# Splitting the weights once: block 0 stores the fp32r pairs in DRAM, and blocks 1 to 3 load them

## The chip, the core and the metric

The kernel runs on one core of one Trainium2 chip. The metric is the device time of one execution in microseconds. Before the change it was 3058.07 us, the median of three runs.

## The reference

One layer of a streaming encoder is applied to 2048 prompt rows and 32 sample rows of width 1024. What matters here is that every row goes through the same weights:

```
h = RMSNorm(x);  proj = h @ w_in          # 1024 x 9760: q k v, gates, z, x B C, dt
branch_a = (window_attention(q, k, v) * silu(g_att)) @ w_attn_o
branch_s = (ssd_scan(conv(xBC), dt) * silu(z), grouped RMSNorm) @ w_ssm_o
out = (sigmoid(ga) * branch_a + sigmoid(gs) * branch_s) @ w_out
x  <- x + RMSNorm(out)
```

## The kernel before

The 2048 rows are cut into four blocks of 512 columns (the tokens lie along the free axis). Block 1 also carries the 32 sample rows, so its matmuls run in two parts of 272 columns. The scan state and the last rows of convolution and keys pass from block to block.

A float32 product is made of three fp32r matmuls: each operand is split into a rounded part (hi) and the rest (lo), and hi*hi, hi*lo and lo*hi are summed in PSUM. The activations are split where they are made. The weights are split by `prep`, in every block again.

The projections of a block are a list of 125 jobs, and the four lists stand one behind the other in `jobs`. A job makes 128 output channels. A *whole job* has eight slices of 128 rows of weights and so 24 matmuls of 512 columns; a *half job* (the 32 jobs of `ssm_out`, which multiply by `w_ssm_o` group by group) has four slices and 12 matmuls. The first job of a block (`dt`, marked `mix`) holds both parts in one tile. `emit_job` writes a job's matmuls on TensorE; `half_of` holds the matmul itself (L142). Everything else, the scan of a group (`load`, `prepare` and `finish` for each chunk of 128 tokens), attention, and the norms, is a list of side steps that `advance` places between the matmuls of the jobs, one step for each whole job or two half jobs.

Each side step takes PSUM tiles from the pool `sd` (four buffers). In the scan, `finish` takes three of them (y0, y, pst) and the `prepare` that follows takes two (pb, ps), so the transposes of x into ps (L437) wait until VectorE has read the y0 of that `finish` (L479, which writes into `ee`).

Weights in the loop over jobs:

```
while done_load < min(nj, j + 1 + LOOK_DMA):    # LOOK_DMA = 4
    load_raw(done_load); done_load += 1
while done_prep < min(nj, j + 1 + LOOK):        # LOOK = 2
    prep(done_prep); done_prep += 1
```

`load_raw` brings 512 KB (a whole job, or two half jobs) into one of three `raw` buffers. `prep` copies it on ScalarE to fp32r (`whi`, L123) and subtracts on VectorE (`wlo`, L127); there are three buffers of each, so the pair of job j+2 can be written only when the matmuls of job j-1 are done. All DMAs are issued by SyncE, one queue in program order: a DMA that waits holds up every DMA behind it. In the scan, `load` brings the chunk's rows of the decay from a small DRAM tile, 512 KB into `rr` and 256 KB into `ee` by two DMAs (three buffers of each), so such a load waits for the `finish` that read the buffer before. The order of each engine's instructions is fixed when the program is built, by the framework's scheduler.

Of the kernel before, what the change touches and what calls it, by code (L numbers as in the profile page):

```python
# [7 lines left out]
F32 = mybir.dt.float32  # L8
F32R = mybir.dt.float32r
# [5 lines left out]
P = 128  # L15
# [14 lines left out]
LOOK_DMA = 4  # L30
# [3 lines left out]
def hybrid_step_kernel(ctx: ExitStack, tc: tile.TileContext, ins, outs):  # L34
# [6 lines left out]
    wp = pool("wp", 3)  # L41
# [4 lines left out]
    sm = pool("sm", 4)  # L46
    dram = pool("dram", 2, space=bass.MemoryType.DRAM)
    mm = pool("mm", 4, space=bass.MemoryType.PSUM)
    sd = pool("sd", 4, space=bass.MemoryType.PSUM)

    act, vec, pl, pe = nc.scalar, nc.vector, nc.gpsimd, nc.tensor
    dma = nc.sync.dma_start

    # ---------------------------------------------------------------- constants
    cst = const.tile([P, 3, P], F32, name="cst")
# [6 lines left out]

    # ---------------------------------------------------------------- state kept over blocks
    H = const.tile([P, 4, 512], F32, name="H")
# [12 lines left out]

    # ---------------------------------------------------------------- helpers
    def rsqrt(x, n, rows=P):
# [14 lines left out]

    # ---------------------------------------------------------------- weights
    jobs = []
    raws = {}

    def raw_key(j):
        return jobs[j]["raw"]  # L100
# [10 lines left out]

    prepped = {}

    def prep(j):
        load_raw(j)
        jb = jobs[j]
        rv = raws[raw_key(j)]
        o = jb["off"]
        kt = jb["load"][1]
        src = rv[:, :, o:o + P]  # L120
        hi = wp.tile([P, 1024], F32R, name="whi")[:, :kt * P].rearrange("p (k c) -> p k c", k=kt)
        lo = None if jb["mix"] else wp.tile([P, 1024], F32R, name="wlo")[:, :kt * P].rearrange("p (k c) -> p k c", k=kt)
        act.activation(hi, src, AF.Copy)  # L123
        if jb["mix"]:
            vec.tensor_tensor(hi[:, :, 32:64], src[:, :, :32], hi[:, :, :32].bitcast(F32), op=ALU.subtract)
        else:
            vec.tensor_tensor(lo, src, hi.bitcast(F32), op=ALU.subtract)  # L127
        prepped[j] = (hi, lo)

# [83 lines left out]

    # ---------------------------------------------------------------- one block
    def block(b):
# [12 lines left out]

        # ---- input norm and transposition
        def stage_a(io):  # L230
# [64 lines left out]

        # ---- dt
        def evac_dt(res):
# [63 lines left out]

        # ---- conv channels
        def evac_conv(ci, dst):
# [32 lines left out]

        # ---- state space scan of one group
        def ssd_steps(g, ph):
# [190 lines left out]

        # ---- attention  # L590
        def att_open(ph):
# [111 lines left out]
        def att_unit(kv, ph):  # L703
# [18 lines left out]
            def softmax(sps, pt, rng_, neg, n):  # L722
                # rng_: per column i the (source AP, destination AP, max group)
                mx = sm.tile([P, 4], F32, name="mx")
# [260 lines left out]

    # ---------------------------------------------------------------- plan
    blocks = [block(b) for b in range(NB)]
# [31 lines left out]
    for b in range(NB):  # L1019
# [57 lines left out]
        add_jobs(w_ou, KT, 0, 8, tb, bk["rhs_m"], [bk["evac_out"](d) for d in range(8)], name=("outs", b))  # L1077
        jobs[-5]["after"].append((f"o{b}", bk["out_steps"](ph)))

    # ---------------------------------------------------------------- run  # L1080
    open_phase("io", 9)()
    for slot in blocks[0]["stage_a"](ph):
        for f in slot:
            f()
    # ---------------------------------------------------------------- small parameters
    load_raw(0)
# [98 lines left out]
    for j in range(nj):  # L1185
# [5 lines left out]
        if "ensure" in jb:  # L1191
            nm, key = jb["ensure"]
            for side in list(active):
                while side[0] == nm and key not in finished:
                    advance(side, True)
        while done_load < min(nj, j + 1 + LOOK_DMA):
            load_raw(done_load)
            done_load += 1
# [79 lines left out]
```

## Time and profile before

| | |
|---|---|
| time, median of 3 runs | 3058.07 us (3057.89 to 3060.25) |
| span of the profiled execution, first to last instruction | 3055.3 us |
| TensorE busy | 2977.4 us |
| VectorE busy | 2146.2 us |
| ScalarE busy | 1445.6 us |
| GpSimd busy | 587.2 us |
| moved by DMA | 323.40 MB, 106 GB/s in the mean |
| granted clock of TensorE, mean | 0.995 |

The span is 2.8 us shorter than the median time; what lies around it is the launch and the end. "Busy" counts the time in which at least one instruction of the engine ran, and the idle time of an engine is the rest of the span. TensorE is idle for 77.9 us of 3055.3.

### The profile page before, as it was taken

What the parts mean: (1) busy time and instruction counts of PE and PEld (TensorE: products, weight loads), DVE (VectorE), ACT (ScalarE), POOL (GpSimd) and SP (SyncE); (2) the same over time, 40 slices, a digit from 0 to 9 for tenths busy, and PEclk for the clock granted to TensorE, in tenths of its full rate; (3) what the DMA queues carried; (4) which work ended last, traced back from release to release, by engine and by line L of the source; (5) the groups of instructions that cost most, each with busy time, mean ns of one, the idle gap of its engine ahead of it and who ended that gap; (6) DMA issues with size and microseconds to landing.
All of it is one profiled execution on the core that took longest, in us unless ns stands there. A gap on an engine that the chain in (4) does not pass through costs nothing. (4 is left out here: it accounts for less than half of the span.)

```text
span 3055.3 us, 47433 instructions
## 1 busy us (share of the span) xinstructions
PE 2977.4 (97%) x17983; PEld 2530.2 (83%) x17983; DVE 2146.2 (70%) x4097; ACT 1445.6 (47%) x3127; POOL 587.2 (19%) x599
## 2 busy tenths in 40 slices
PE   8999999999999999999999999999999999999998
PEld 7777877788999999989997777877788777887787
DVE  7888777644888877774557878777357778777634
ACT  5555435533556444454345554355335454435522
POOL 2323210001343322000103322200011322220000
PEclk9999999999999999999999999999999999999999
DMA  6343332334534333223335343322445443332332
GB/s 174 104 121 106 98 95 75 90 107 131 141 105 123 93 104 102 70 57 111 118 107 140 108 120 104 97 83 63 124 124 149 108 124 105 102 101 77 91 105 76
DMA packets 549726, 323.40 MB, mean 106 GB/s; under 512 B 19000, under 2 KB 538520, under 8 KB 549496
## 3 DMA queue, kind: packets, MB, share of 16 engines
q1 hardware_dynamic: 549496, 320.35, 37.4%
q8 instruction: 142, 2.33, 0.3%
q14 instruction: 88, 0.72, 0.1%
HBM read 308.99 MB, written 11.32 MB: 105 GB/s over the span
## 5 line engine op out<-in xcount | busy, mean ns | idle before, releaser
L142 PE MATMUL mm<-hhi,whi 128*128 128x512 f32 (+2 forms) x3104 | 1103.0, 356 | 0.6 <-ACT hhi L253 0.6
L142 PE MATMUL mm<-hlo,whi 128*128 128x512 f32 (+2 forms) x3104 | 1093.1, 353 | 0.6 <-DVE hlo L254 0.6
L142 PE MATMUL mm<-hhi,wlo 128*128 128x512 f32 (+2 forms) x3056 | 1081.4, 354 | 0.2 <-DVE wlo L127 0.2
L127 DVE TENSOR_TENSOR wlo<-raw,whi 128x1024 fp32r<-128x1024 f32 (+1 forms) x496 | 597.7, 1205 | 409.6 <-ACT whi L123 393.4
L123 ACT ACTIVATE whi<-raw 128x1024 fp32r<-128x1024 f32 (+1 forms) x500 | 474.3, 949 | 702.5 <-PE mm L142 570.1
L142 PEld LDWEIGHTS mm<-hhi,whi 128*128 128x128 f32 x3104 | 586.2, 189 | 89.1 <-issue 11.1
L142 PEld LDWEIGHTS mm<-hlo,whi 128*128 128x128 f32 x3104 | 586.7, 189 | 76.4 <-DVE hlo L254 0.8
L142 PEld LDWEIGHTS mm<-hhi,wlo 128*128 128x128 f32 x3056 | 576.8, 189 | 77.1 <-issue 0.5
L142 PE MATMUL mm<-u,whi 128*128 128x512 f32 (+1 forms) x1920 | 511.4, 353 | 0.0
L142 PEld LDWEIGHTS mm<-u,whi 128*128 128x128 f32 x1920 | 335.3, 188 | 51.9 <-issue 2.2
L142 PE MATMUL mm<-u,wlo 128*128 128x512 f32 (+1 forms) x960 | 338.6, 353 | 0.5 <-DVE wlo L127 0.5
L441 ACT ACTIVATE rr<-rr,ncum 128x128 f32<-128x128 f32 (+1 forms) x544 | 170.3, 386 | 110.0 <-POOL rr L438 110.0
L378 DVE SCALAR_TENSOR_TENSOR u<-xp,par,u 128x512 f32<-128x512 f32 (+1 forms) x240 | 184.7, 791 | 25.7 <-ACT u L375 25.3
L142 PEld LDWEIGHTS mm<-u,wlo 128*128 128x128 f32 x960 | 180.4, 188 | 24.9 <-DVE wlo L127 0.7
L880 POOL TENSOR_TENSOR s<-s,S 128x512 f32<-128x512 f32 (+1 forms) x32 | 51.3, 1602 | 631.2 <-ACT whi L123 365.8
L734 ACT ACTIVATE pt<-sd,nm 128x192 f32<-128x192 f32 (+3 forms) x260 | 104.9, 412 | 122.8 <-DVE nm L728 111.6
L620 POOL TENSOR_TENSOR s<-s,cs 128x512 f32<-128x512 f32 (+1 forms) x40 | 55.3, 1383 | 465.4 <-DVE s L618 452.4
L380 POOL COPY halo<-xp 128x3 f32<-128x3 f32 x96 | 50.2, 523 | 455.4 <-ACT xp L372 455.4
L438 POOL TENSOR_SCALAR_AFFINE_SELECT rr<-rr 128x1024 f32<-128x1024 f32 (+1 forms) x68 | 86.9, 1277 | 239.4 <-DMA rr<-cd 220.3
L142 PE MATMUL mm<-tA,whi 128*128 128x512 f32 (+2 forms) x344 | 117.2, 341 | 0.1
L142 PE MATMUL mm<-S,whi 128*128 128x512 f32 (+2 forms) x344 | 116.5, 339 | 0.4 <-DVE S L884 0.4
L142 PE MATMUL mm<-tA,wlo 128*128 128x512 f32 (+2 forms) x344 | 116.3, 339 | 0.0
(251 smaller groups left out, 4044.2 us busy)
## 6 DMA issues: line engine op xcount, KB each, us to landing
raw<-in_w_in_dram SPq DMA_DIRECT2D x308, 512.0 KB
rr<-cd SPq DMA_DIRECT2D x64, 512.0 KB
raw<-in_w_ssm_o_dram SPq DMA_DIRECT2D x64, 512.0 KB
ee<-cd SPq DMA_DIRECT2D x128, 128.0 KB
raw<-in_w_attn_o_dram SPq DMA_DIRECT2D x32, 512.0 KB
raw<-in_w_out_dram SPq DMA_DIRECT2D x32, 512.0 KB
x<-in_x_prompt_dram SPq DMA_DIRECT2D x24, 512.0 KB
out_dram<-u SPq DMA_DIRECT2D x12, 512.0 KB
```

The costliest lines, as they stand in the source:

```text
L123: act.activation(hi, src, AF.Copy)
L127: vec.tensor_tensor(lo, src, hi.bitcast(F32), op=ALU.subtract)
L142: last_mm[0] = pe.matmul(ps, w[:, k, :], r(k, n0, n), start=k == 0 and i == 0, stop=k == kt - 1 and i == len(ops) - 1)
L378: vec.scalar_tensor_tensor(o[:, d0:d0 + n], xp[:, off + t:off + t + n], convw[:, t, ci:ci + 1], o[:, d0:d0 + n], op0=ALU.mult, op1=ALU.add)
L380: pl.tensor_copy(halo[:, :, ci], xp[:, BT:BT + 3])
L438: pl.affine_select(w[:q, :, :q], w[:q, :, :q], pattern=[[0, 8], [1, q]], compare_op=ALU.is_ge, fill=-1e30, base=0, channel_multiplier=-1)
L441: act.activation(w[:q, h, :q], w[:q, h, :q], AF.Exp, scale=1.0, bias=ncum[:q, co + g * 8 + h:co + g * 8 + h + 1])
L620: pl.tensor_tensor(sh[:, :tb], sh[:, :tb], cs[:, 1, :tb], op=ALU.mult)
L734: act.activation(dst, src, AF.Exp, bias=nm[:, i:i + 1], scale=0.125, accum_out=den[:, i:i + 1])
L880: pl.tensor_tensor(m[:, :tb], m[:, :tb], s[:, :tb], op=ALU.add)
```

## The change

`prep` now has two ways. In block 0 it loads and splits as before, but the two parts lie in one tile `w` of 8 KB for each partition, and a DMA copies that tile to a DRAM tile `wd` of the job's own. For a job of blocks 1 to 3 `prep` is one DMA that brings the stored pair of the same job of block 0 into `w`: 1 MB for a whole job, 512 KB for a half job and for `dt`. `w` has three buffers, as `whi` and `wlo` had. The raw loads end with block 0.

```diff
+    wdram = pool("wdram", 1, space=bass.MemoryType.DRAM)
...
+    per_block = [0]
...
+    held = {}
 
     def prep(j):
+        jb = jobs[j]
+        kt = jb["load"][1]
+        m = kt * P
+        w = wp.tile([P, 2048], F32R, name="w")
+        hi, lo = (w[:, i * m:(i + 1) * m].rearrange("p (k c) -> p k c", k=kt) for i in range(2))
+        used = w[:, :m] if jb["mix"] else w[:, :2 * m]
+        prepped[j] = (hi, None if jb["mix"] else lo)
+        if j >= per_block[0]:
+            dma(used.bitcast(F32), held[j % per_block[0]])
+            return
         load_raw(j)
-        jb = jobs[j]
-        rv = raws[raw_key(j)]
         o = jb["off"]
-        kt = jb["load"][1]
-        src = rv[:, :, o:o + P]
-        hi = wp.tile([P, 1024], F32R, name="whi")[:, :kt * P].rearrange("p (k c) -> p k c", k=kt)
-        lo = None if jb["mix"] else wp.tile([P, 1024], F32R, name="wlo")[:, :kt * P].rearrange("p (k c) -> p k c", k=kt)
+        src = raws[raw_key(j)][:, :, o:o + P]
         act.activation(hi, src, AF.Copy)
...
-        prepped[j] = (hi, lo)
+        held[j] = wdram.tile([P, used.shape[1]], F32, name=f"wd{j}")
+        dma(held[j], used.bitcast(F32))
...
+        if b == 0:
+            per_block[0] = len(jobs)
...
-        while done_load < min(nj, j + 1 + LOOK_DMA):
+        while done_load < min(per_block[0], j + 1 + LOOK_DMA):
```

The scheduler also places other instructions anew. VectorE, block 3, group 0, at the `finish` of the second chunk (L479 reads its y0; L458 is the last step of the `prepare` ahead; L378 and L385 are the convolution of the next group; L481 to L487 end the `finish` of the first chunk). Before:

```order
L484 TENSOR_TENSOR u<-u 128x4x128
L447 SCALAR_TENSOR_TENSOR bl<-sd,bh 128x128
L449 TENSOR_TENSOR xd<-sd,dth 128x512
L458 SCALAR_TENSOR_TENSOR rr<-rr,sd 128x1024
L378 SCALAR_TENSOR_TENSOR u<-xp,par,u 128x512
L127 TENSOR_TENSOR wlo<-raw,whi 128x1024
L378 SCALAR_TENSOR_TENSOR u<-xp,par,u 128x512
L479 TENSOR_TENSOR ee<-sd,ee 128x512
```

The same place with the change, where each line stands nine further down (L479 is L488, L458 is L467, L378 is L387):

```order
L493 TENSOR_TENSOR u<-u 128x4x128
L456 SCALAR_TENSOR_TENSOR bl<-sd,bh 128x128
L458 TENSOR_TENSOR xd<-sd,dth 128x512
L467 SCALAR_TENSOR_TENSOR rr<-rr,sd 128x1024
L488 TENSOR_TENSOR ee<-sd,ee 128x512
L387 SCALAR_TENSOR_TENSOR u<-xp,par,u 128x512
```

The split and the two convolution steps no longer stand between L458 and L479. It is so at all six such places of blocks 2 and 3 (the second chunk of groups 0, 1 and 2); in block 0 all three keep the order of before, and in block 1 six L378 stay ahead of L479 and only the split goes.

SyncE, block 1, around the write of the sample's scan state of group 2 (`out_9`), which falls into the half jobs 43 to 50. Before, with raw loads for later jobs around it:

```order
L413 DMA rr_11478<-cd_7133 128x8x128
L109 DMA raw_10925<-in_w_in_dram 128x8x128
L416 DMA ee_11480<-cd_7133 64x4x128 x2
L495 DMA out_9_dram<-s2_10849 128x4x128
L109 DMA raw_10959<-in_w_in_dram 128x8x128
```

The same place with the change (`wd49` is the stored pair of job 49):

```order
L126 DMA w_10760<-wd48_2894 128x1024
L422 DMA rr_11387<-cd_7234 128x8x128
L425 DMA ee_11389<-cd_7234 64x4x128 x2
L504 DMA out_9_dram<-s2_10794 128x4x128
L126 DMA w_10836<-wd49_2915 128x1024
L126 DMA w_10866<-wd50_2936 128x1024
```

Before, what stood behind the state's write were loads of raw weights that are split jobs later; now it is the pair of the job after the next.

## Rows read from the trace of the kernel before

**Rows 1.** The page: busy us (share of the span) and instructions of each engine.

```profile
PE 2977.4 (97%) x17983; PEld 2530.2 (83%) x17983; DVE 2146.2 (70%) x4097; ACT 1445.6 (47%) x3127; POOL 587.2 (19%) x599
```

**Rows 2.** Busy time by stage: blocks 0 to 3, and the end.

```profile
core 0: us, PE busy (x) PEld busy (x) DVE busy (x) ACT busy (x) POOL busy (x), PEclk, DMA share, GB/s
0.00:760.00 760.00, 735.33 (x3856) 594.88 (x3857) 530.56 (x989) 360.06 (x749) 141.57 (x142) 1.00 0.39 110
760.00:1530.00 770.00, 753.31 (x6232) 727.18 (x6231) 562.98 (x1191) 379.78 (x915) 171.72 (x192) 1.00 0.37 103
1530.00:2300.00 770.00, 757.10 (x4044) 616.74 (x4042) 530.75 (x982) 359.28 (x744) 140.15 (x134) 1.00 0.38 107
2300.00:3043.40 743.40, 730.59 (x3851) 590.78 (x3850) 514.72 (x918) 344.08 (x714) 131.99 (x130) 1.00 0.37 102
```

**Rows 3.** The page: the two groups of the weight split.

```profile
L127 DVE TENSOR_TENSOR wlo<-raw,whi 128x1024 fp32r<-128x1024 f32 (+1 forms) x496 | 597.7, 1205 | 409.6 <-ACT whi L123 393.4
L123 ACT ACTIVATE whi<-raw 128x1024 fp32r<-128x1024 f32 (+1 forms) x500 | 474.3, 949 | 702.5 <-PE mm L142 570.1
```

**Rows 4.** TensorE's waits in block 1: us in total, times, longest us.

```profile
PE sd L437 <- DVE ee L479: 5.8, 3, 2.7
PE sd L778 <- DVE pt L738: 4.1, 6, 1.1
PE sd L492 <- DVE s L487: 1.7, 1, 1.7
PE sd L659 <- ACT s L651: 1.3, 1, 1.3
```

**Rows 5.** TensorE's waits in blocks 2 and 3.

```profile
PE sd L437 <- DVE ee L479: 16.3, 6, 3.5
PE sd L468 <- DVE H L487: 4.0, 6, 2.1
PE sd L528 <- POOL s L518: 3.0, 2, 2.5
```

**Rows 6.** TensorE's waits in block 0.

```profile
PE sd L437 <- DVE ee L479: 7.6, 3, 3.2
PE sd L468 <- DVE H L487: 2.1, 2, 1.4
```

**Rows 7.** Timeline, block 3, one such wait: start us, us, instruction [idle before <-releaser].

```profile
2379.34 0.37 SPq L413 DMA_DIRECT2D rr<-cd  x1
...
2384.21 1.71 POOL L438 TENSOR_SCALAR_AFFINE_SELECT rr<-rr 128x1024 f32<-128x1024 f32 x1 [4.62 <-DMA rr<-cd]
...
2385.96 2.44 ACT L441 ACTIVATE rr<-rr,ncum 128x128 f32<-128x128 f32 x8 [2.29 <-POOL rr L438]
...
2387.19 1.20 DVE L458 SCALAR_TENSOR_TENSOR rr<-rr,sd 128x1024 f32<-128x1024 f32 x1
...
2388.31 1.04 ACT L123 ACTIVATE whi<-raw 128x1024 fp32r<-128x1024 f32 x1
...
2390.54 0.75 DVE L378 SCALAR_TENSOR_TENSOR u<-xp,par,u 128x512 f32<-128x512 f32 x1 [2.14 <-ACT u L375]
...
2391.20 2.31 DVE L127 TENSOR_TENSOR wlo<-raw,whi 128x1024 fp32r<-128x1024 f32 x1
...
2394.93 0.68 DVE L479 TENSOR_TENSOR ee<-sd,ee 128x512 f32<-128x512 f32 x1
...
2395.67 0.55 PE L437 MATMUL sd<-cst,u 128*128 128x128 f32 x3 [3.23 <-DVE ee L479]
```

**Rows 8.** The chain that ended last: one whole job without side steps.

```profile
2224.32 5.59 PE mm L142 x24
```

**Rows 9.** Timeline at the start: a load of 512 KB and its first reader.

```profile
0.74 0.39 SPq L241 DMA_DIRECT2D x<-in_x_prompt_dram  x1
...
4.27 1.06 ACT L242 ACTIVATE u<-x 128x1024 f32<-128x1024 f32 x1 [2.25 <-DMA x<-in_x_prompt_dram]
```

**Rows 10.** One microsecond of DMA each: a raw load, and a write of rows.

```profile
472.00:473.00 1.00, 1.00 (x6) 0.79 (x5) 0.88 (x3) 0.96 (x1) 0.00 (x0) 1.00 1.13 338
761.50:762.50 1.00, 1.00 (x10) 0.95 (x11) 0.97 (x4) 0.94 (x4) 0.00 (x0) 1.00 1.06 422
```

**Rows 11.** Timeline, block 1, the state's write of group 2 and TensorE's job 49.

```profile
1070.84 0.29 PE L142 MATMUL mm<-u,wlo 128*128 128x272 f32 x1
...
1076.81 0.39 SPq L495 DMA_DIRECT2D out_dram<-s  x1
...
1077.43 0.41 PE L142 MATMUL mm<-u,whi 128*128 128x272 f32 x2
```

**Rows 12.** The page: the loads that carry weights.

```profile
raw<-in_w_in_dram SPq DMA_DIRECT2D x308, 512.0 KB
raw<-in_w_ssm_o_dram SPq DMA_DIRECT2D x64, 512.0 KB
raw<-in_w_attn_o_dram SPq DMA_DIRECT2D x32, 512.0 KB
raw<-in_w_out_dram SPq DMA_DIRECT2D x32, 512.0 KB
```

## The prediction

> **What bounds the kernel now.** I read the page's busy times first. TensorE works for 2977.4 us of the span of 3055.3, 97%; VectorE for 70%, ScalarE for 47% [rows 1]. The change takes nothing from TensorE, so the next question is what its 77.9 idle us are. The table by stage splits them: 760.00 - 735.33 = 24.7 us in block 0, 16.7 in block 1, 12.9 in block 2, 12.8 in block 3, and the rest after the last matmul [rows 2]. Only blocks 1 to 3 lose their splits, so the change can win at most 16.7 + 12.9 + 12.8 = 42 us. That is 1.4% of the time, however much work goes from the other engines.
>
> Who ends those waits stands in TensorE's waits by block. In blocks 2 and 3, 16.3 us in six waits are those of the transposes L437 for VectorE's L479, the reader of the PSUM tile that they need [rows 5]. The same wait costs 5.8 us in block 1, beside 4.1 for the softmax (L738) and 1.7 and 1.3 for two single places [rows 4], and 7.6 us in block 0 [rows 6]. One of the six, read in the timeline, shows the mechanism. VectorE ends L458 at 2388.39 and could then read y0. In its queue the next instruction is L378, which waits until 2390.54 for ScalarE, and ScalarE is late because it waited for the rr rows from DRAM (asked for at 2379.34, taken up by GpSimd at 2384.21), then did eight exponentials (2.44 us), then a weight split (1.04 us). Behind L378 come the other half of the split (2.31 us) and a second L378, and L479 runs at 2394.93. TensorE stood for 3.23 us [rows 7].
>
> **The change, part by part.**
>
> *Splits removed.* 375 of the 500 copies and three quarters of the subtractions go: 0.75 x 474.3 = 356 us of ScalarE and 0.75 x 597.7 = 448 us of VectorE [rows 3]. Neither engine is the bound, so these 804 us are worth what they take from TensorE's waits, and I go by place:
> - The six L437 waits of blocks 2 and 3: with the change L479 stands directly behind L458. In the timeline that is 2388.39 instead of 2394.93, 6.5 us earlier, against a wait of 3.23 [rows 7]. The y0 it reads is there by then. I count all 16.3 us [rows 5], 16 in round numbers.
> - The L437 waits of block 1 keep six convolution steps ahead of L479; one subtraction (1.2 us) leaves VectorE's queue and one copy (0.95 us) ScalarE's ahead of each of the three [rows 3]. I count some 1.3 us for each, 4 of the 5.8 us [rows 4].
> - The softmax waits of block 1 (4.1 us in six): a split stands in the queue of some of them; I take 2.5. The two single waits L492 and L659 (3.0 us) are for engines that lose splits; I take 2 [rows 4].
> - L468 (4.0 us) and L528 (3.0 us) of blocks 2 and 3 hang on the rr rows, the squares and GpSimd, not on a split [rows 5]: I take 2 of the 7.
>
> The sum is 16 + 4 + 2.5 + 2 + 2 = 26.5, say 27 us. The bounds are 0 (each wait finds another late partner) and 42.
>
> *Writes added in block 0.* 92 whole jobs at 1 MiB and 33 at half that make 108.5 MiB = 113.8 MB. Large rows went at 422 GB/s [rows 10], so that is 270 us of all DMA engines beside the 0.39 x 760 us = 296 us of now [rows 2]: 566 of 760, still no bound. But the rr load is issued behind such a write, and block 0 keeps the old VectorE order, in which each of the five waits of rows 6 hangs on rr. The write is 1.05 MB / 422 GB/s = 2.5 us; the raw load that rr shares the engines with today does the same in part, 0.52 MB / 338 GB/s = 1.6 us [rows 10]. I take 1.2 us for each of the five, 6 us. The bounds are 0, and 2.5 us at all five, 12.5. SyncE also holds each write until the split is done; behind it in the queue stand the raw load for three jobs on and the scan's loads, none of them due sooner than a whole job of 5.59 us [rows 8].
>
> *Loads of pairs in blocks 1 to 3.* The traffic: raw weights were 436 loads of 0.524 MB, 228.6 MB [rows 12]; now 57.2 raw and 3 x 113.8 = 341.3 of pairs are read. The mean of blocks 1 to 3 goes from about 104 GB/s to about 177, far under 422. What counts is the delay. A pair can be asked for only when job j-3 ends, and is needed when j begins, two jobs later: 2 x 5.59 = 11.2 us for whole jobs, 5.6 for half jobs [rows 8]. No row shows a load of 1 MB. A load of 512 KB took 3.53 us from issue to its reader (0.74 to 4.27) with others beside it [rows 9], and 4.87 with a raw load beside it (2379.34 to 2384.21 [rows 7]). One of 1 MB then takes 3.5 + 1.25 = 4.8 us at best and 4.9 + 1.25 = 6.1 at worst. I take 4.8, the row with large rows being nearer. All whole jobs are covered by 11.2 us, and half jobs by 5.6.
>
> Covered, if SyncE is free to ask. It isn't everywhere: the state's write of group 2 waits for ScalarE until 1076.81, with the pair of job 49 behind it. That buffer was free from 1071.1 (the last matmul of job 46 starts at 1070.84), and job 49 begins at 1077.43 [rows 11]. Asked for at 1077.2 and there some 3 us later, it stops TensorE for about 2.5 us, and what waits behind TensorE is the whole program. The like of it stands at the two or three state writes of block 3 that fall into half jobs, and at the out rows at the start of a block. I take 6 us for all of them. The bounds are 0 (ScalarE has no more splits and writes the state sooner) and 20 (every join from half to whole jobs, 4 in a block, late by the 0.5 us that 6.1 exceeds 5.6, for two jobs each, 12 us, and the 6 and some more).
>
> *The sum.* On the span: 3055.3 - 27 + 6 + 6 = 3040.3; with the 2.8 us around it, **3043 us** against a median of 3058.07, 0.5% less.
>
> **The rivals.**
>
> *All waits go.* If nothing new comes late, the time is 3058.1 - 42 = 3016. For it: VectorE and ScalarE fall to about half of their load in blocks 1 to 3. Against: 7 us of the waits are tied to GpSimd and rr [rows 5], and the state writes are there.
>
> *The waits only change owner* (the change doesn't do what it says). The rr rows and the eight exponentials stay as they are, and they opened the wait of rows 7; pairs of 1 MB now share the DMA engines with rr at up to 2.5 us each. If half of the 27 us come back so, the time is 3058.1 - 13.5 + 6 + 6 = 3057, no change. Against: in blocks 2 and 3 L479 is no longer behind anything that waits for ScalarE's next job.
>
> *Slower: half jobs starve.* If the time L from "buffer free" to "pair there" exceeds 5.6 us in the half jobs, three buffers hold one load for every two jobs, a job lasts L / 2, and 96 half jobs of blocks 1 to 3 lose L / 2 - 2.8 us each. At L = 6.5 that is 43 us: 3058.1 - 27 + 6 + 43 = 3080. It makes the kernel slower by over 0.2% from L = 6.2 on. For it: 4.87 us is already on record for a shared load [rows 7], and SyncE adds its own queue. Against: half jobs have half loads, and in most of them there is no scan beside.
> The Trainium skill (DMA: Bandwidth & Descriptors, section Measured) lists 6.15 us for a transfer of 1 MB of its kind; by it the whole-job pairs that follow half jobs would come about 0.6 us late, eight in a block, some 14 us over three blocks. The Trainium skill gives on the same page, section Anatomy of one DMA, 2.0 us plus bytes over 436 GB/s, 4.4 us for 1 MB, by which none is late; no run so far shows which holds here.
>
> *Slower: block 0.* If every one of its 16 rr loads is late by 2.5 us and TensorE waits each time, block 0 loses 40 us in place of 6: 3077. It would need 1.7 us at each chunk to end slower than before by over 0.2%; only five of them are waited for today [rows 6].
>
> **How the numbers follow.** About 0.2% (6 us) is what a measurement of this kernel can tell from no change. The forecast, with 3030 to 3052 as its own range, has a chance of 0.48; all waits go 0.12; change of owner 0.22; starving half jobs 0.12; block 0 0.06. Faster by over 0.2% is then 0.48 + 0.12 = 0.60, within it 0.22, slower 0.18. The range runs from 3022, inside the case in which all waits go, to 3068, past the unchanged time and into the beginning of the slower cases; some 0.05 lie below and 0.13 above.
>
> **What would show each step.** Right: in blocks 2 and 3 the wait of L437 for L479 is nearly gone (16.3 us before), VectorE is busy for about 1700 us and ScalarE for about 1090, and TensorE's idle time of blocks 1 to 3 falls from 42 to some 20 us. Block 0 has some 6 us more idle time, on the same L437. New waits of the matmuls L142 for the DMA of w appear at few places, first at job 49 of block 1, a few us in all. Wrong: waits of L142 for w spread over the half jobs (starving); L437 waits of the old size with another releaser (change of owner); block 0 longer by 20 us or more.

## The result, and the profile after

The changed kernel takes 3021.26 us (median of four runs, 3019.91 to 3023.18) against 3057.98 us of the kernel before in the same comparison. The ratio is 0.9885, with an interval of 0.9873 to 0.9896: 1.15% faster, a gain of 36.7 us where 15 were forecast, and 0.7 us below the lower end of the range.

The page of the changed kernel, busy time of each engine (answers to [rows 1]):

```profile
PE 2969.7 (98%) x17983; PEld 2527.1 (84%) x17983; DVE 1733.8 (57%) x3722; ACT 1128.8 (37%) x2752; POOL 502.7 (17%) x599
```

The span is 3018.1 us, 37.2 less than before. VectorE lost 412 us and ScalarE 317, somewhat less than the 448 and 356 counted for the splits. TensorE's idle time fell from 77.9 to 48.4 us, by 29.5. The other 7.7 us came out of its *busy* time (2977.4 to 2969.7) at the same 17983 matmuls. What they are is shown by TensorE's clock, below.

Its table by stage, cut where its own blocks begin (answers to [rows 2]):

```profile
core 0: us, PE busy (x) PEld busy (x) DVE busy (x) ACT busy (x) POOL busy (x), PEclk, DMA share, GB/s
0.00:748.50 748.50, 730.06 (x3805) 589.33 (x3806) 525.75 (x970) 353.58 (x739) 135.24 (x142) 1.00 0.80 262
748.50:1555.00 806.50, 798.51 (x6602) 773.28 (x6600) 443.43 (x1093) 293.34 (x827) 138.50 (x193) 1.00 0.52 173
1555.00:2278.50 723.50, 720.01 (x3757) 580.65 (x3755) 385.64 (x847) 241.93 (x594) 113.60 (x133) 1.00 0.56 188
2278.50:3006.30 727.80, 720.02 (x3822) 583.16 (x3821) 371.75 (x794) 237.57 (x589) 113.67 (x130) 1.00 0.55 183
```

Idle TensorE time is now 18.4, 8.0, 3.5 and 7.8 us. In the kernel before, the first matmuls of blocks 1, 2 and 3 start at 753.5, 1569.5 and 2306.7 us and the last one ends at 3043.4; now these are 748.5, 1555.0, 2278.5 and 3006.3. So the blocks gained 5.0, 9.5, 13.7 and 8.9 us. **Block 0, which keeps all its splits and has the writes on top, is faster.** The DMA engines are busy for 0.80 of it, at 262 GB/s.

TensorE's waits of the changed kernel in block 0 (two rows, answers to [rows 6]):

```profile
PE sd L477 <- DVE H L496: 3.6, 4, 2.3
...
PE sd L446 <- DVE ee L488: 0.2, 1, 0.2
```

In block 1 (answers to [rows 4]):

```profile
PE sd L446 <- DVE u L490: 2.4, 3, 0.9
PE sd L787 <- DVE pt L747: 1.9, 3, 1.1
...
PE sd L446 <- DVE ee L488: 0.7, 1, 0.7
```

In blocks 2 and 3 (answers to [rows 5]):

```profile
PE sd L501 <- DVE H L496: 4.8, 3, 2.5
PE sd L477 <- DVE H L496: 3.8, 5, 1.4
PE mm L151 <- DMA w<-wd: 1.4, 2, 1.3
```

L437, now L446, waited 29.7 us for VectorE's L479 in the whole kernel; L446 waits 1.0 us for L488. The waits for w are 1.4 us in all. New are 4.8 us at the state's transposes L501 in block 3.

The timeline of the place of [rows 7] in the changed kernel (start us, us, instruction, idle before it and its releaser):

```profile
2357.47 1.21 DVE L467 SCALAR_TENSOR_TENSOR rr<-rr,sd 128x1024 f32<-128x1024 f32 x1
...
2359.17 0.69 DVE L488 TENSOR_TENSOR ee<-sd,ee 128x512 f32<-128x512 f32 x1 [0.49 <-PE sd L477]
...
2359.36 0.56 ACT L381 COPY xp<-mm 128x512 f32<-128x512 f32 x1
...
2360.63 0.76 DVE L387 SCALAR_TENSOR_TENSOR u<-xp,par,u 128x512 f32<-128x512 f32 x1 [0.77 <-ACT u L384]
...
2363.99 0.60 PE L446 MATMUL sd<-cst,u 128*128 128x128 f32 x4
```

This is as forecast: L488 stands behind L467, waits only for the matmuls that make its y0, and the four transposes L446 run 4.1 us after its end without a wait. ScalarE is still late there: five of the eight exponentials stand ahead of the convolution's copy L381 and wait 2.48 us for rr, and L387 waits 0.77 us for ScalarE. Only L488 no longer stands behind any of it.

**The clock behind the waits.** In the kernel before, TensorE's granted clock is at half, 1.2 instead of 2.4 GHz, for 3.4 us at the end of or just behind each of its seven longest L437 waits (2.6 to 3.5 us); these stretches begin at 106.7, 185.2, 932.7, 1659.8, 1738.3, 2397.0 and 2475.5 us. One of them, in block 2: the wait, two matmuls in the stretch, two behind it, and the stretch itself with its PEclk of 0.50 (columns as in [rows 2]):

```profile
1658.82 0.66 PE L437 MATMUL sd<-cst,u 128*128 128x128 f32 x4 [3.51 <-DVE ee L479]
...
1660.22 0.63 PE L142 MATMUL mm<-hhi,whi 128*128 128x512 f32 x1
1660.65 0.63 PE L142 MATMUL mm<-hlo,whi 128*128 128x512 f32 x1
...
1663.42 0.39 PE L142 MATMUL mm<-hhi,wlo 128*128 128x512 f32 x1
1663.66 0.39 PE L142 MATMUL mm<-hhi,whi 128*128 128x512 f32 x1
```

```profile
1659.75:1663.16 3.41, 3.41 (x9) 2.63 (x8) 3.41 (x8) 2.39 (x8) 0.00 (x0) 0.50 0.02 7
```

In the stretch a matmul begins every 0.43 us, behind it every 0.23. So such a stretch costs about 3.4 x (1 - 0.23 / 0.43) = 1.6 us, an estimate from these rows, and all of it is listed as busy. The changed kernel has two such stretches once its clock has risen at the start, neither at a wait of L446 (which is L437):

```profile
174.12:177.53 3.41, 3.41 (x21) 2.79 (x21) 3.41 (x6) 0.63 (x1) 2.00 (x2) 0.50 1.02 241
867.02:870.43 3.41, 3.41 (x18) 3.41 (x17) 2.58 (x7) 1.89 (x7) 0.32 (x2) 0.50 0.86 322
```

Five fewer make some 8 us by that estimate. Against it stands the start: the clock rises at 20.5 us, in the kernel before at 14.5, and matmuls of 256 columns begin every 0.21 us there instead of every 0.12, which costs block 0 an estimated 2 us. In blocks 1 to 3 busy time fell by 9.0 us, of which four stretches fewer are some 6; the rest is open.

Block 0 was forecast the other way. The kernel before, there, at the second chunk of group 0:

```profile
96.69 2.45 ACT L441 ACTIVATE rr<-rr,ncum 128x128 f32<-128x128 f32 x8 [2.24 <-POOL rr L438]
...
99.99 0.57 ACT L372 COPY xp<-mm 128x512 f32<-128x512 f32 x1
...
101.27 0.76 DVE L378 SCALAR_TENSOR_TENSOR u<-xp,par,u 128x512 f32<-128x512 f32 x1 [2.15 <-ACT u L375]
...
105.68 0.68 DVE L479 TENSOR_TENSOR ee<-sd,ee 128x512 f32<-128x512 f32 x1
...
106.41 0.90 PE L437 MATMUL sd<-cst,u 128*128 128x128 f32 x4 [3.20 <-DVE ee L479]
```

The same place in the changed kernel:

```profile
99.21 0.59 ACT L381 COPY xp<-mm 128x512 f32<-128x512 f32 x1 [2.03 <-PE mm L151]
...
100.37 1.05 ACT L131 ACTIVATE w<-raw 128x1024 fp32r<-128x1024 f32 x1
...
100.89 0.74 DVE L387 SCALAR_TENSOR_TENSOR u<-xp,par,u 128x512 f32<-128x512 f32 x1
...
104.40 0.68 DVE L488 TENSOR_TENSOR ee<-sd,ee 128x512 f32<-128x512 f32 x1
...
105.13 0.66 PE L446 MATMUL sd<-cst,u 128*128 128x128 f32 x4
...
107.06 2.45 ACT L450 ACTIVATE rr<-rr,ncum 128x128 f32<-128x128 f32 x8 [0.66 <-POOL rr L447]
```

VectorE's order is the old one: a convolution step, the split, two more, then L488. But on **ScalarE** the eight exponentials of this chunk (the fourth of group 0) and the copy of the split no longer stand ahead of the convolution's copies. Before, ScalarE waited 2.24 us for the masked rr rows, did eight exponentials and a split, and only then freed the convolution (L372). Now the exponentials stand behind the same copy, at 107.06, and the split's copy behind it at 100.37. L381 waits for its own matmuls alone, VectorE's L387 doesn't wait at all, and neither does TensorE.

### The profile page after: what moved, and what is told of

It is laid out like the page before. It is cut to its first block, busy times and chain, and to the rows that moved or that the text cites. A ratio compares the mean times of both kernels' runs of the same rounds, so it can differ in the third digit from the quotient of the medians.

```text
span 3018.1 us, 46690 instructions
## 1 busy us (share of the span) xinstructions
PE 2969.7 (98%) x17983; PEld 2527.1 (84%) x17983; DVE 1733.8 (57%) x3722; ACT 1128.8 (37%) x2752; POOL 502.7 (17%) x599
## 4 chain that ended last, share of the span: by engine, by line
PE 56%; DVE 4%; DMA 3%; ACT 2%; issue 1%; POOL 1%; SPq 0%; DVEq 0%; POOLq 0%; ACTq 0%
PE mm L151 49%; DMA rr<-cd 2%; PE sd L804 1%; PE sd L787 1%; PE sd L481 1%; DVE u L387 1%; PE sd L477 1%; PE sd L765 1%; PE sd L485 1%; PE sd L766 1%; ACT rr L450 1%; DMA w<-wd 1%; POOL rr L447 1%; PE sd L446 0%; PE sd L920 0%
## 5 line engine op out<-in xcount | busy, mean ns | idle before, releaser
L151 PE MATMUL mm<-hhi,w 128*128 128x512 f32 (+2 forms) x6160 | 1673.6, 354 | 2.4 <-DMA w<-wd 1.3
L151 PEld LDWEIGHTS mm<-hhi,w 128*128 128x128 f32 x6160 | 1082.6, 188 | 167.0 <-issue 12.1
L151 PE MATMUL mm<-hlo,w 128*128 128x512 f32 (+2 forms) x3104 | 1091.0, 352 | 0.4 <-DVE hlo L263 0.4
L151 PEld LDWEIGHTS mm<-hlo,w 128*128 128x128 f32 x3104 | 586.0, 189 | 75.6 <-DVE hlo L263 0.7
L151 PE MATMUL mm<-u,w 128*128 128x512 f32 (+1 forms) x2880 | 567.6, 353 | 0.2 <-DMA w<-wd 0.2
L151 PEld LDWEIGHTS mm<-u,w 128*128 128x128 f32 x2880 | 467.3, 188 | 76.6 <-issue 2.8
L387 DVE SCALAR_TENSOR_TENSOR u<-xp,par,u 128x512 f32<-128x512 f32 (+1 forms) x240 | 172.8, 743 | 43.9 <-ACT u L384 43.4
L135 DVE TENSOR_TENSOR w<-raw,w 128x1024 fp32r<-128x1024 f32 (+1 forms) x124 | 147.1, 1187 | 64.9 <-ACT w L131 64.4
L151 PE MATMUL mm<-tA,w 128*128 128x512 f32 (+2 forms) x688 | 174.0, 340 | 0.1
L131 ACT ACTIVATE w<-raw 128x1024 fp32r<-128x1024 f32 (+1 forms) x125 | 118.5, 948 | 62.5 <-PE mm L151 46.4
L151 PEld LDWEIGHTS mm<-tA,w 128*128 128x128 f32 x688 | 118.3, 188 | 14.2 <-ACT tA L892 0.3
L381 ACT COPY xp<-mm 128x512 f32<-128x512 f32 (+1 forms) x120 | 59.1, 493 | 175.9 <-PE mm L151 172.3
```

The lines of the kernel that those rows point to most:

```text
L151: last_mm[0] = pe.matmul(ps, w[:, k, :], r(k, n0, n), start=k == 0 and i == 0, stop=k == kt - 1 and i == len(ops) - 1)
L381: act.copy(xp[:, 3 + n0:3 + n0 + m], ps[:, :m])
L387: vec.scalar_tensor_tensor(o[:, d0:d0 + n], xp[:, off + t:off + t + n], convw[:, t, ci:ci + 1], o[:, d0:d0 + n], op0=ALU.mult, op1=ALU.add)
```

## The experiments

Two theories were set against each other. **Freed time**: the 804 us taken from VectorE and ScalarE end the waits. **Order**: ScalarE's place in the row for rr's exponentials and the split ends them, and that place changed as a by-product. All ratios are to the kernel before, run beside them on the same chip; their intervals are about 0.0012 (3.7 us) to each side, unless one is given.

**1. The pairs are written and never read.**

```diff
-        if j >= per_block[0]:
-            dma(used.bitcast(F32), held[j % per_block[0]])
-            return
...
+        if j < per_block[0]:
+            held[j] = wdram.tile([P, used.shape[1]], F32, name=f"wd{j}")
+            dma(held[j], used.bitcast(F32))
...
-        while done_load < min(per_block[0], j + 1 + LOOK_DMA):
+        while done_load < min(nj, j + 1 + LOOK_DMA):
```

> Block 0 as in the changed kernel (one tile for the pair, the pair written to DRAM); blocks 1 to 3 as before, with raw loads and both splits, so the stored pairs are never read. Order theory (in block 0 ScalarE's exponentials of the late rr rows, L441 before, now stand behind the next job's two copies of the convolution, L372 and L375, instead of ahead of them): block 1 starts about 5 us sooner than the 753.5 us of the kernel before, as it did in the changed kernel (748.5), and blocks 1 to 3 lose and gain nothing, so about 3053 us. Freed-time theory (only the work taken from VectorE and ScalarE ends waits; block 0's gain came from elsewhere): nothing is freed here, so 3058 us. The step of the prediction by which the writes delay rr in block 0: 6 us more, 3064 us, with the L437 waits of block 0 longer than the 7.6 us of before.

Measured: 3041.19 us, ratio 0.9951 (0.9939 to 0.9964). No work is gone, 113.8 MB of writes are added, and the kernel is 15 us faster. Block 0 gained 5.2 us as the order theory has it, but blocks 2 and 3 gained 7.2 and 6.6 that no theory had. In those blocks its waits for what is L479 before fell from 16.3 us [rows 5] to this:

```profile
PE sd L444 <- DVE ee L486: 3.0, 6, 0.8
```

There ScalarE's copy of the split stands behind the next job's convolution copies, and before it stood ahead of them, as in [rows 7] (L123 at 2388.31). The step of the prediction by which the writes cost 6 us falls.

**2. The removed work put back, with no reader.** In the branch of blocks 1 to 3:

```diff
             dma(used.bitcast(F32), held[j % per_block[0]])
+            src = used[:, :m].bitcast(F32)
+            ja = wp.tile([P, 1024], F32, name="raw", bufs=3)[:, :m]
+            act.activation(ja.bitcast(F32R), src, AF.Copy)
+            jv = wp.tile([P, 1024], F32, name="raw", bufs=3)[:, :m // 4 if jb["mix"] else m]
+            vec.tensor_tensor(jv.bitcast(F32R), src[:, :jv.shape[1]], ja[:, :jv.shape[1]], op=ALU.subtract)
             return
```

> The changed kernel, and in blocks 1 to 3, behind each load of a pair, the two operations of the split once more, of the same sizes, from the loaded pair into buffers that nobody reads; the matmuls use the loaded pair, so they wait for no split. Freed-time theory: VectorE is back at about 2150 us and ScalarE at about 1445, and 32 us of the 37 gained (all but block 0's 5) are lost: about 3053 us. Order theory (ScalarE's exponentials behind the convolution's copies, and a matmul that waits for no split): most of the gain of blocks 1 to 3 stays, about 3028 us.

Measured: 3049.41 us, ratio 0.9976 (0.9967 to 0.9986). 28 of the 37 us are lost again, near the freed-time theory's 32. Freed time isn't the only difference: with the extra work the scheduler also puts two to four instructions between L467 and L488 at several chunks of blocks 2 and 3 where the changed kernel has none or one.

**3. The kernel before, with rr's exponentials kept in the program's order.** The one edit, which takes no work away:

```diff
-                        act.activation(w[:q, h, :q], w[:q, h, :q], AF.Exp, scale=1.0,
-                                       bias=ncum[:q, co + g * 8 + h:co + g * 8 + h + 1])
+                        tc.keep_in_program_order(act.activation(
+                            w[:q, h, :q], w[:q, h, :q], AF.Exp, scale=1.0,
+                            bias=ncum[:q, co + g * 8 + h:co + g * 8 + h + 1]))
```

> The kernel before with one edit: the scan's exponentials of rr (L441) keep their place in the program's order, which puts them on ScalarE behind the convolution's two copies of the next job, where the changed kernel has them in block 0. No work is removed and nothing is written to DRAM; VectorE's order stays as before. Order theory: each block gains what block 0 gained in the changed kernel, 5 us, so about 3038 us, with the L437 waits of before (29.7 us in 12) mostly gone. Freed-time theory: no change, 3058 us.

Measured: 3020.9 us, ratio 0.9882 (0.9866 to 0.9897), **the same as the whole change**. The order theory's 3038 was too small, and freed time as the only cause is out: this kernel has all its splits, as its page shows.

```profile
PE 2970.2 (98%) x17983; PEld 2523.0 (84%) x17983; DVE 2145.1 (71%) x4097; ACT 1446.2 (48%) x3127; POOL 596.2 (20%) x599
```

The place of [rows 7] in this kernel:

```profile
2360.18 1.20 DVE L459 SCALAR_TENSOR_TENSOR rr<-rr,sd 128x1024 f32<-128x1024 f32 x1
...
2361.61 0.75 DVE L378 SCALAR_TENSOR_TENSOR u<-xp,par,u 128x512 f32<-128x512 f32 x1 [0.22 <-ACT u L375]
...
2361.99 2.45 ACT L441 ACTIVATE rr<-rr,ncum 128x128 f32<-128x128 f32 x8
...
2362.28 2.33 DVE L127 TENSOR_TENSOR wlo<-raw,whi 128x1024 fp32r<-128x1024 f32 x1
...
2365.19 0.67 DVE L480 TENSOR_TENSOR ee<-sd,ee 128x512 f32<-128x512 f32 x1
...
2365.92 0.66 PE L437 MATMUL sd<-cst,u 128*128 128x128 f32 x4 [0.49 <-DVE ee L480]
```

The split and two convolution steps still stand between L459 and L480. But the first L378 waits 0.22 us for ScalarE instead of 2.14, the exponentials run behind the copies without waiting for rr, and the transposes wait 0.49 us instead of 3.23. What held VectorE was ScalarE's wait for rr, not the split. Why the order theory's gain was too small is in part the clock: of the seven stretches at half clock one is left (at 1150.1 us), and six fewer make an estimated 9.6 of the 37 us, where the theory had counted idle time alone.

**4. The changed kernel with the same edit.**

> The changed kernel with the same edit as the one before this: the exponentials of rr keep their place in the program's order. Order theory: the waits of the transposes for VectorE are gone already, so about 3021 us, at best 3 us less. Freed-time theory: 3021 us. If the exponentials come later than they need, the state's matmuls wait for them: up to 3030 us.

Measured: 3004.85 us, ratio 0.9833 (0.982 to 0.9846), the fastest of all: 1.67% under the kernel before. Both theories' 3021 was wrong; the two remedies add up in part. Its blocks 2 and 3:

```profile
1554.30:2274.60 720.30, 719.00 (x3757) 581.02 (x3756) 388.34 (x847) 241.75 (x594) 112.46 (x133) 1.00 0.56 189
2274.60:2994.70 720.10, 718.86 (x3822) 583.54 (x3821) 372.34 (x794) 237.78 (x589) 111.20 (x130) 1.00 0.56 185
```

TensorE is idle for 1.3 and 1.2 us in them.

**5 and 6. The price of loads and of stores, with the exponentials in order.** Experiment 5 is experiment 2 and experiment 6 is experiment 1, each with the edit of experiment 3.

> The changed kernel with the exponentials of rr kept in the program's order, and in blocks 1 to 3 a copy on ScalarE and a subtraction on VectorE of the split's sizes from each loaded pair into buffers that nobody reads. Against the kernel before with the exponentials in order (3020.9 us) it has the same work on VectorE and ScalarE, and the stores and loads of pairs besides; against the changed kernel with them in order (3004.85 us) it has 804 us more of work on the two engines. Freed-time theory (the 16 us between these two are the worth of the removed work): about 3021 us. Order theory (what the removed work was worth is that VectorE's order got free of the convolution between L467 and L488, and that stays in part here): about 3010 us. If loads and stores of pairs cost what the prediction took for them, 12 us, they show here as time above 3021: 3033 us.

> The kernel that writes the pairs of block 0 and never loads them, with the exponentials of rr in the program's order. Beside the kernel before with the same order (3020.9 us) it has only the 113.8 MB of writes in block 0 and the one tile for a pair more. The step of the prediction by which the writes make rr late in block 0: 6 us more, 3027 us. If the exponentials no longer meet a late rr, the writes are hidden: 3021 us, with block 1 starting at 745 to 749 us.

Measured: experiment 5 3041.18 us (0.995, 0.9938 to 0.9962), experiment 6 3023.4 us (0.9893, 0.988 to 0.9906). The stores cost 3.4 us by the ratios (0.9893 against 0.9882), which the intervals don't tell from nothing. Experiment 5 is a miss: none of its three numbers. It loses 36 us to the kernel of experiment 4. TensorE's waits there are spread (6.8 us for the softmax in block 1, 4.7 for w in blocks 2 and 3), and at one chunk of each of blocks 2 and 3 eleven instructions stand between L459's and L480's counterparts. So the splits without a reader don't price the real ones.

**7. More bytes of loads, and 8. half of them.** Experiment 7, on the kernel of experiment 4:

```diff
+            dma(wp.tile([P, 1024], F32, name="raw", bufs=3)[:, :m], held[j % per_block[0]][:, :m])
             dma(used.bitcast(F32), held[j % per_block[0]])
```

> The changed kernel with the exponentials of rr in order (3004.85 us), and in blocks 1 to 3, ahead of each load of a pair, a load of the pair's first half into a buffer that nobody reads: 1.5 times the bytes of pairs (170 MB more), each pair asked for one DMA later. If the loads have the slack that two jobs give them (the changed kernel shows only 1.4 us of waits for w), about 3007 us. The step of the prediction by which pairs are asked for too late at the state's writes and the joins, and the rival by which half jobs starve (a pair there more than 5.6 us after its buffer came free): each pair comes about 1.5 us later, so the 96 half jobs lose 0.75 us each once the slack is gone, up to 72 us: 3020 to 3075 us.

Measured: 3037.81 us, ratio 0.9941 (0.9929 to 0.9953). The time lies in the expected range of late pairs (3020 to 3075), but the edit doesn't do what it was to do, which was to make each pair one DMA later. The scheduler issued the added loads, which nobody reads, far ahead: 8 of the 375 fall into block 0, 261 into block 1, 106 into block 2 and none into block 3. Its table for blocks 1 and 2, and TensorE's longest wait in block 1:

```profile
747.40:1576.10 828.70, 806.20 (x6602) 781.44 (x6599) 442.07 (x1093) 292.20 (x827) 140.86 (x193) 0.99 0.90 313
1576.10:2303.60 727.50, 720.74 (x3758) 580.36 (x3756) 388.82 (x847) 241.95 (x594) 115.35 (x133) 1.00 0.74 253
```

```profile
PE mm L152 <- DMA w<-wd: 17.4, 6, 5.1
```

Block 1, at 313 GB/s and a DMA share of 0.90, is 23 us longer than in experiment 4 (805.7); block 2, at 0.74, 7.2 longer; block 3, without added loads, lasts 720.1 us as there. So loads of pairs came late where the added loads were, and the changed kernel, at a share of 0.52 to 0.56, shows nearly none of it. Whether the full engines or the added loads ahead of each pair in the queue made them late is not told apart, and five of the six waits stand at whole jobs, so the price of late pairs at half jobs is not tested.

Experiment 8, on the kernel of experiment 4; it leaves out the stored rest of each weight, so it doesn't compute the layer:

```diff
-            dma(used.bitcast(F32), held[j % per_block[0]])
+            dma(hi.bitcast(F32), held[j % per_block[0]].rearrange("p (k c) -> p k c", k=kt))
+            prepped[j] = (hi, None if jb["mix"] else hi)
...
-        held[j] = wdram.tile([P, used.shape[1]], F32, name=f"wd{j}")
-        dma(held[j], used.bitcast(F32))
+        held[j] = wdram.tile([P, m], F32, name=f"wd{j}")
+        dma(held[j], used[:, :m].bitcast(F32))
```

> The changed kernel with the exponentials of rr in order (3004.85 us), but only the rounded half of each pair is written in block 0 and loaded in blocks 1 to 3 (half of the bytes both ways), and the matmuls of blocks 1 to 3 use it for the rest as well, so the third product is not that of the reference; the count and shape of all matmuls are the same. What the bytes of pairs still cost shows as time below 3005. The prediction's step (6 us for late pairs, 6 for the writes): about 2996 us. If both are hidden, as the waits for w (1.4 us) and block 0 say: 3003 to 3005 us.

Measured: 3012.72 us, ratio 0.9856 (0.9842 to 0.9871), 8 us *slower* than with full pairs. By the starts of the blocks, 4.6 us of that are lost in blocks 0 and 1, where the split of block 0 is now waited for (2.5 us in three places); blocks 2 and 3 last 720.6 and 721.1 us against 720.3 and 720.1. Half of the bytes buys nothing there, so in blocks 2 and 3 the loads are hidden. Why block 0 lost is open.

**9. One tile for the pair, no store.** Experiment 1 without its stores:

```diff
-        if j < per_block[0]:
-            held[j] = wdram.tile([P, used.shape[1]], F32, name=f"wd{j}")
-            dma(held[j], used.bitcast(F32))
```

> The kernel before with one edit: the two parts of a pair lie in one tile w instead of whi and wlo. Nothing is written to DRAM, nothing is loaded ready, all four blocks split. In all blocks ScalarE's copy of the split then stands behind the next job's two convolution copies; the eight exponentials of rr stay ahead of these. Order theory: the part of the gain of the kernel that stores and never loads (3041.2 us) which fell into blocks 1 to 3 (1.1, 7.2 and 6.6 us) comes from this place in the queue alone, and block 0 gains some 3 us: 3038 to 3043 us. If the stores made that gain: 3058 us.

Measured: 3045.09 us, ratio 0.9964 (0.9952 to 0.9977). A change of the tile alone, with no DMA and no instruction more or less, gains 11 us. Its order of ScalarE in blocks 1 to 3 is that of experiment 1. Blocks 2 and 3 gained 2.0 and 4.0 us here and 7.2 and 6.6 there; with the same order I take this for the spread of single executions (this kernel's runs lie between 3041.6 and 3051.8). The 4 us between experiments 9 and 1 are within their intervals.

**10. The kernel before, with the split's copy kept in the program's order.**

```diff
-        act.activation(hi, src, AF.Copy)
+        tc.keep_in_program_order(act.activation(hi, src, AF.Copy))
```

> The kernel before with one edit: ScalarE's copy of the split (L123) keeps its place in the program's order; two tiles, no store. In the scan it then stands ahead of the exponentials of rr and no longer between these and the convolution's copies, and on VectorE the subtraction leaves the place between L458 and L479 at most chunks. Order theory: gain of some 10 to 20 us, 3038 to 3048 us. Freed-time theory: no work is gone, 3058 us. At the second chunk of group 1 fourteen instructions stand between L458 and L479; if that place costs a wait of 5 us in each block, 20 us are lost again, 3058 us or more.

Measured: 3072.89 us, ratio 1.0053 (1.0039 to 1.0067), *slower* by 16 us. The place with fourteen instructions did not decide it. Two of the waits of TensorE:

```profile
PE sd L468 <- DVE H L487: 14.2, 25, 1.6
PE mm L142 <- ACT whi L123: 14.0, 5, 5.9
```

The waits of L437 for L479 are down to 0.3 us, but now the matmuls wait for the splits themselves (5.9 us once in block 0, at 48.44 us, and some 2 us once in each block), and L468 waits 25 times. At four of these waits for splits the clock falls to half (from 47.4, 320.4, 1091.8 and 1873.5 us). To end one wait is no gain if another takes its place.

**11 and 12. Half of the work put back.** Experiment 2 with the copy on ScalarE alone, and with the subtraction on VectorE alone (from the loaded pair).

```diff
             dma(used.bitcast(F32), held[j % per_block[0]])
+            src = used[:, :m].bitcast(F32)
+            ja = wp.tile([P, 1024], F32, name="raw", bufs=3)[:, :m]
+            act.activation(ja.bitcast(F32R), src, AF.Copy)
             return
```

```diff
             dma(used.bitcast(F32), held[j % per_block[0]])
+            src = used[:, :m].bitcast(F32)
+            ja = src
+            jv = wp.tile([P, 1024], F32, name="raw", bufs=3)[:, :m // 4 if jb["mix"] else m]
+            vec.tensor_tensor(jv.bitcast(F32R), src[:, :jv.shape[1]], ja[:, :jv.shape[1]], op=ALU.subtract)
             return
```

> The changed kernel, and in blocks 1 to 3 a copy on ScalarE of the split's size from each loaded pair into a buffer that nobody reads. VectorE has no split back, and its order is that of the changed kernel. If ScalarE's time is what ended the waits, some 15 us of the 20 that loading in place of splitting is worth (3041.2 to 3021.3 us) are lost: about 3036 us. If it was VectorE's time and order: 3021 to 3024 us.

> The changed kernel, and in blocks 1 to 3 a subtraction on VectorE of the split's size from each loaded pair into a buffer that nobody reads; ScalarE has no copy back. If VectorE's time and order are what loading in place of splitting is worth: about 3041 us or more, as much as with both operations back (3049.4 us). If ScalarE's: 3021 to 3026 us.

Measured: experiment 11 3025.47 us (0.9901, 0.9886 to 0.9915), experiment 12 3030.8 us (0.9915, 0.9896 to 0.9933; its runs spread over 16 us). By the ratios ScalarE's work back costs 5 us, which the intervals don't tell from nothing, VectorE's 9, and both together 28. Neither engine's time alone carries the gain of loading.

## Why the prediction was right and wrong

What the runs give as a sum, by ratios to the kernel before times 3058 us:

| step | free order | exponentials in order |
|---|---|---|
| kernel before | 0 | -36.1 (3) |
| one tile for the pair | -11.0 (9) | |
| and stores in block 0 | -15.0 (1) | -32.7 (6) |
| and loads in place of splits: the change | -35.2 | -51.1 (4) |

To load in place of splitting is worth 20.2 us in the left column and 18.4 in the right one. To store, with the tile that it needs, is worth -15.0 on the left and costs 3.4 on the right.

- **The first step that failed is "Writes added in block 0": "block 0 keeps the old VectorE order, in which each of the five waits of rows 6 hangs on rr", at a price of 6 us.** VectorE's order was read and is indeed kept; ScalarE's was not read, and it is ScalarE that waited for rr. The edits to `prep` changed its row: the single tile put the split's copy behind the convolution's copies in every block that splits (experiment 9), and with the stores the exponentials of rr went behind them as well in block 0. Block 0 gained 5.0 us instead of losing 6, and L437's 7.6 us there fell to 0.2.
- **The second step that failed is "the change can win at most 16.7 + 12.9 + 12.8 = 42 us": it counts a wait as its idle time alone.** Blocks 1 to 3 gained 32.1 us: 23.1 of idle time, and 9.0 that had stood as busy time. Behind five of their waits TensorE had run at half clock; in the changed kernel one such stretch is left there (867.0). Four fewer are some 6 of the 9.0 us by the estimate above. A mean granted clock of 0.995 stood in the table of the kernel before. In experiment 4 the same blocks gained 43.8 us, more than the bound. The Trainium skill (Perfetto Trace Analysis, section Identifying the Most-Contended Engine) says that matmul busy time is no good measure of how close a kernel is to its roofline, because matmuls are pipelined. The trace agrees that it is no measure of work, with 7.7 us less of it at the same count of matmuls; here the larger part of that is the clock.
- **The mechanism of blocks 2 and 3 was right, but the removed work was not needed for it.** "With the change L479 stands directly behind L458" came true and the 16.3 us are gone, though ScalarE still waits for rr there. The forecast booked them under "Splits removed". Experiments 1 and 3 keep all splits, with three instructions still between the two at these places, and end most of these waits, because ScalarE frees the convolution in time. The timeline of [rows 7] showed this other way out: L378 waited 2.14 us for ScalarE, and the prediction said so. That ScalarE's wait for rr is left in the changed kernel fits the 16 us that experiment 4 won beyond it; wait by wait this was not traced.
- **The net idle time of blocks 1 to 3 was about right, in part by luck.** 27 us of waits less 6 for late pairs were to go. Idle time there fell from 42.4 to 19.3 us, by 23.1, and the text had named "some 20 us" as what remains. Block 1 fits by its terms: of the 12.9 us of [rows 4] 8.5 were to go; 10.3 went, and 2.4 came anew (L446 for L490). But in blocks 2 and 3, of the 7 us of L468 and L528, 2 were to go; there are now 3.8 at L477 and 4.8 new ones at L501, so 1.6 more. That miss and the one of the late pairs (6 forecast, 1.4 measured) nearly cancel.
- **Late pairs: 6 us forecast, 1.4 measured.** The place named, job 49 of block 1, has no wait, because the state's write came sooner. SyncE's rows there:

```profile
1062.30 0.40 SPq L504 DMA_DIRECT2D out_dram<-s  x1
1062.79 2.96 SPq L126 DMA_DIRECT2D w<-wd  x2
```

  ScalarE made that state 14.5 us earlier than in [rows 11], the whole program some 9 us earlier at that place (job 49 begins at 1068.2 instead of 1077.4). The lower bound, "ScalarE has no more splits and writes the state sooner", was the right one. The only pair that is waited for by over 0.3 us is that of a whole job behind half jobs:

```profile
1751.24 0.47 PE L151 MATMUL mm<-hhi,w 128*128 128x512 f32 x1 [1.28 <-DMA w<-wd]
```

  This is a join of the kind that the rival *half jobs starve* spoke of, and there is one, where some 24 were possible. Its pair was asked for here and landed 7.2 us later:

```profile
1743.87 0.32 SPq L126 DMA_DIRECT2D w<-wd  x1
```

  By the trace's semaphore records that is an exception: the 276 pairs of 1 MB landed 4.8 us after they were asked for in the median, as the forecast took it, and 32 of them after more than 6.1. The Trainium skill (DMA: Bandwidth & Descriptors) has figures for DMAs that GpSimd issues: by the 6.15 us of its section Measured those joins would have cost an estimated 14 us, by an estimate of 4.4 us from its section Anatomy of one DMA nothing. The trace, with DMAs from SyncE, is nearer to the second: a median of 4.8 us, and 1.4 us of waits.
- **The rivals.** *All waits go* (3016) came nearest in size, for another reason than it gave. *Change of owner* is seen in a small part: 4.8 us at the state's transposes in block 3, which experiment 4 doesn't have. Of the two slower ones the runs show nothing beyond the one join.

The 22 us between forecast and gain are thus 11 in block 0 (+6 forecast, -5.0 measured), and 11 in blocks 1 to 3 (21 forecast, 32.1 measured, of which 9.0 had been counted as busy, most of them by the estimate at half clock).

Open is why experiments 11, 12 and 2 don't add (5, 9 and 28 us): each addition also moves other instructions, so freed time and free places in the queue were not told apart within the 20 us of loading; that part of the gain has no shown cause. That the single tile is what moves the split's copy is shown; by which of its rules the scheduler does so was not tried.

## What to carry to other kernels

When a change edits the code around a scheduler, read the new order of every engine on the path of the wait, above all of the engine that waited first; a by-product (here a tile and a store) can be worth as much as the work removed. An instruction that waits for a DMA on an in-order engine should stand behind everything that is ready: one such edit, kept in the program's order, gave 36 us without removing any work, as much as the whole change, and 51 together with it. But pinning is no rule: pinning the split's copy lost 16 us, so look at what will wait next. And price a wait of TensorE with what follows it: here each of the seven longest L437 waits took an estimated 1.6 us more at half clock, which a table of busy and idle time doesn't show.

## What the hardware showed beside

GpSimd's busy time fell from 587.2 to 502.7 us though its 599 instructions are the same. With ScalarE's copies put back (experiment 11) it is 497.8, with VectorE's subtractions (12) 547.0, with both (2) 577.3: it goes with VectorE's work. In the timeline of [rows 7] VectorE's subtraction L127 took 2.31 us at 2391.20, and 1.22 at 2378.32, where it began first. GpSimd in the kernel before, at these two places:

```profile
2378.83 0.77 POOL L380 COPY halo<-xp 128x3 f32<-128x3 f32 x1 [8.50 <-ACT xp L372]
...
2389.89 0.19 POOL L380 COPY halo<-xp 128x3 f32<-128x3 f32 x1 [1.49 <-ACT xp L372]
2391.10 1.33 POOL L457 TENSOR_TENSOR xl<-s,xh 128x512 fp32r<-128x512 f32 x1 [1.03 <-ACT xh L456]
```

L457 ends at 2392.43, and L127 1.08 us after that: about the time of the subtraction alone, begun when GpSimd had finished. At 2378.83 it is GpSimd that waits: its small copy takes 0.77 us, to 2379.60, when L127 has just ended, and 0.19 where VectorE has nothing of the kind. The Trainium skill (SBUF — State Buffer, section SBUF: two separate sides) says that VectorE instructions with two SBUF inputs and GpSimd instructions that read SBUF take a shared port pair in turn for a whole instruction. The trace agrees. So each removed subtraction also took away one that GpSimd could collide with; what that is worth to TensorE was not measured by itself.
